# RWKV scan on one core: the inversion's matrix is made ahead of the other latent products, the two halves of a join run together, and the first heads' output projection stands ahead of the last chain

## The chip, the core and the metric

The kernel runs on one core of a Trainium2 chip. A core has five engines that each take their instructions in a fixed order: TensorE (PE in the profile; PEld is its loading of weights), VectorE (DVE), ScalarE (ACT), GpSimd (POOL) and SyncE (SP, which issues most of the transfers). The metric is the time of one execution in microseconds (us) on the device; lower is better.

## The reference

Two transformer blocks of two layers each, at 256 tokens by 1024 channels, all in float32; the second block also has 256 context tokens. The change concerns one mixer of the second block's last layer, the RWKV-7 scan over 16 heads of 64 channels, with a context part and then a latent part, in both directions:

```python
def rwkv7_scan(r, w, k, v, kk, a, S):
    def step(S, inp):
        rt, wt, kt, vt, kkt, at = inp
        sa = jnp.einsum("bhvk,bhk->bhv", S, -kkt)
        S = S * wt[:, :, None, :] + sa[..., None] * (kkt * at)[:, :, None, :] + vt[..., None] * kt[:, :, None, :]
        return S, jnp.einsum("bhvk,bhk->bhv", S, rt)
    S, ys = lax.scan(step, S, xs)

def rwkv_out(y, p, kvec, lnx, w_o):
    y = head_layernorm(from_heads(y), lnx[0], lnx[1], RW_HEADS, r.dtype)
    bonus = jnp.sum((r * k * kvec[2]).reshape(bn, L, RW_HEADS, RW_HEAD), axis=-1, keepdims=True) * v...
    return ((y + bonus.reshape(bn, L, D)) * g) @ w_o
```

The latent scan of each direction starts from that direction's final context state. Only the latent output goes on (`need_ctx` is false in the last layer).

## The kernel before

The scan is computed in chunks of 64 tokens. With N the strictly triangular 64x64 matrix of a chunk's keys against their own decayed keys, the chunk needs the inverse of (1 + N). The 16 heads go in four batches, g = 0 to 3, of four heads: two planes (`pl`) of 128 channels, each with two heads. A batch has 64 such matrices (4 heads, 2 directions, 4 chunks, context and latent). Its stages are:

- `prepare(lat)`, for the context (lat 0) and then the latent part (lat 1). `scaled_keys` makes the decays and the scaled keys: small matmuls at L1561, L1575 and L1578 with 64 or fewer rows, a tanh, a scan on VectorE, two exponentials, and elementwise products. `products` then makes, in runs of 64x64 matmuls at L1626, the keys against the rates (one kind gives N, copied by ScalarE at L1633 into the tile XN, the other kind gives A12, masked by VectorE at L1632), for the latent part also the keys against the receptances (masked by VectorE into AL, L1645), and the keys by token (transposes, copied by ScalarE into BT, L1648). `values` transposes the values (L1661) into SV (L1664). The latent part also makes the bonus (L1590 to L1593).
- `invert_blocks`: two copies on ScalarE (L1678), a transpose on VectorE (L1680, tile `ul`), and 62 VectorE operations (L1688, L1690) that invert all 32x32 diagonal blocks of the batch at once. It reads XN of both parts alone.
- `join_blocks`: the blocks are joined to inverses of 64x64 by two rounds of 32x32 matmuls (L1712, L1717), each with copies behind it (L1714, L1719), first for one half of the units, then for the other. Ahead of it ScalarE moves the off-diagonal blocks (L1701).
- `chain(lat)`: four steps, each of which waits for the one before: matmul pp (L1753), copy P, matmul pu (L1760), copies SV on ScalarE and VectorE (L1762), matmul pd (L1765), scaling on VectorE (L1769). The latent chain also adds up the output py (L1742).
- `output`: head layer norm, bonus and gate (L1786 to L1812).

At the end `finish` multiplies by `w_o`: weights are loaded and split into a high and a low part (L209 on ScalarE, L210 on VectorE), and each of 8 output tiles is a sum of matmuls of three products (L242, L243, L244). The first six chunks of channels (batches 0 to 2) are summed early, 8 times 18 matmuls; the last two after batch 3's output.

The order on each engine comes from the Tile framework: it emits instructions by priority, which is the order of the program unless a block is wrapped in `C.early(mark)`, and takes one that is ready by its own plan. So the order is fixed when the kernel is built. The program's order was: all of batch g+1's `prepare(0)`, then batch g's chain(0), `prepare(1)` of g+1, then the inversion of g+1 with chain(1) of g wrapped early, the join, the output of g. `finish` is emitted after both chains of batch 3. PSUM has two banks for the small matmuls (`psm`), two for products, joins and the projection (`ptr`), and one each for the chain's pp, pu, pd and py.

## Time and profile before

| | before |
|---|---|
| median of 3 runs | 2874.9 us (2871.64 to 2876.14) |
| profiled execution | 2889.15 us |
| its span, first to last instruction | 2887.3 us |
| granted TensorE clock, mean of the span | 0.914 |
| busy: TensorE, VectorE, ScalarE | 90%, 72%, 45% of the span |
| the RWKV scan, from batch 0's first key to batch 3's output | 2137.3 to 2652.8 us |

The median is of runs without the profiler; the rows below are all from the one profiled execution, so lengths of stages are to be held against 2889.15. A granted clock of 1.00 is TensorE's 2.4 GHz, 0.50 is 1.2 GHz; a mean between them is a mix of both.

### The profile page before, as it was taken

How to read it: one execution, taken by the hardware profiler on the slowest of the kernel's cores; microseconds unless marked ns; L12 is line 12 of the kernel's file. 1: busy time of each engine (PE TensorE's matmuls, PEld its weight loads, DVE VectorE, ACT ScalarE, POOL GpSimd, SP SyncE). 2: the span in 40 equal slices, each digit the busy share in tenths (PEclk: the TensorE clock that was granted, in tenths of full speed). 3: DMA queues.
4: the chain of work that ended last, by engine and by line, in shares of the span. 5: the costliest groups of instructions: out<-in, count | busy, mean ns of one | idle time of the engine just before them, and what ended most of it. 6: DMA issues, size and time to landing. Idle time of an engine off the chain costs nothing. (4 is left out here: it accounts for less than half of the span.)

```text
span 2887.3 us, 52999 instructions
## 1 busy us (share of the span) xinstructions
PE 2602.2 (90%) x21548; PEld 2303.9 (80%) x21548; DVE 2065.4 (72%) x4032; ACT 1286.7 (45%) x2237; POOL 632.1 (22%) x417
## 2 busy tenths in 40 slices
PE   8988989999989999899996999897995887788898
PEld 8987889999978899887865877676873766665898
DVE  7785877877866888555438997987858576733993
ACT  5443454444444454346444432335753343322564
POOL 1042320220333301320104212123012010101443
PEclk9998999999989999999986999998995876866899
DMA  7663236666643266521102445432320000011454
GB/s 243 210 217 99 88 112 215 212 214 202 219 156 103 90 211 212 168 88 45 52 30 83 134 153 188 162 117 97 122 75 14 9 18 9 28 38 44 146 187 135
DMA packets 315891, 356.86 MB, mean 124 GB/s; under 512 B 9088, under 2 KB 294016, under 8 KB 315520
## 3 DMA queue, kind: packets, MB, share of 16 engines
q1 hardware_dynamic: 315648, 353.47, 37.7%
q8 instruction: 170, 2.79, 0.4%
q14 instruction: 73, 0.60, 0.1%
HBM read 348.20 MB, written 5.24 MB: 122 GB/s over the span
## 5 line engine op out<-in xcount | busy, mean ns | idle before, releaser
L242 PE MATMUL pmm<-x,hi 128*128 128x256 f32 (+1 forms) x2944 | 927.3, 317 | 39.3 <-ACT hi L209 9.8
L243 PE MATMUL pmm<-x,hi 128*128 128x256 f32 (+1 forms) x2944 | 921.3, 313 | 9.2 <-DVE x L920 5.7
L244 PE MATMUL pmm<-x,lo 128*128 128x256 f32 (+1 forms) x2944 | 918.3, 312 | 1.9 <-DVE lo L210 1.9
L209 ACT ACTIVATE hi<-raw 128x1024 fp32r<-128x1024 f32 (+3 forms) x572 | 570.6, 1002 | 706.5 <-PE pmm L243 406.6
L210 POOL TENSOR_TENSOR lo<-raw,hi 128x1024 fp32r<-128x1024 f32 (+3 forms) x191 | 443.9, 2325 | 1448.5 <-ACT hi L209 1358.3
L242 PEld LDWEIGHTS pmm<-x,hi 128*128 128x128 f32 x2944 | 563.6, 192 | 84.7 <-issue 16.4
L210 DVE TENSOR_TENSOR lo<-raw,hi 128x1024 fp32r<-128x1024 f32 (+2 forms) x381 | 475.8, 1250 | 200.1 <-ACT hi L209 197.9
L243 PEld LDWEIGHTS pmm<-x,hi 128*128 128x128 f32 x2944 | 562.8, 191 | 49.7 <-DVE x L920 8.0
L244 PEld LDWEIGHTS pmm<-x,lo 128*128 128x128 f32 x2944 | 563.0, 191 | 38.9 <-issue 4.2
L242 PE MATMUL pmm<-ah,hi 128*128 128x256 f32 (+1 forms) x1056 | 319.6, 303 | 16.0 <-DVE X L332 11.7
L244 PE MATMUL pmm<-ah,lo 128*128 128x256 f32 (+1 forms) x1056 | 318.9, 302 | 2.5 <-DVE lo L210 2.5
L243 PE MATMUL pmm<-al,hi 128*128 128x256 f32 (+1 forms) x1056 | 318.3, 301 | 0.0
L242 PEld LDWEIGHTS pmm<-ah,hi 128*128 128x128 f32 x1056 | 201.6, 191 | 25.8 <-issue 18.1
L882 DVE SCALAR_TENSOR_TENSOR modp<-wmod,cond 128x512 bf16<-128x512 f32 (+1 forms) x210 | 199.3, 949 | 27.4 <-DMA wmod<-in_w_mod_dram 25.7
L244 PEld LDWEIGHTS pmm<-ah,lo 128*128 128x128 f32 x1056 | 201.5, 191 | 10.8 <-DVE lo L210 3.0
L243 PEld LDWEIGHTS pmm<-al,hi 128*128 128x128 f32 x1056 | 201.7, 191 | 7.8
L1280 DVE SCALAR_TENSOR_TENSOR cv<-pmm,vecs,cv 128x189 f32<-128x189 f32 (+3 forms) x396 | 154.5, 431 | 1.9
L882 DVE SCALAR_TENSOR_TENSOR modp<-wmod,X 128x1024 bf16<-128x1024 f32 x78 | 114.6, 1470 | 23.8 <-DMA wmod<-in_w_mod_dram 22.7
L283 PE MATMUL pmm<-hi,x 128*128 128x256 f32 x224 | 67.9, 303 | 0.0
L1294 ACT ACTIVATE cv<-cv 128x512 f32<-128x512 f32 (+1 forms) x44 | 22.9, 524 | 99.6 <-DVE cv L1280 99.5
L285 PE MATMUL pmm<-lo,x 128*128 128x256 f32 x224 | 66.6, 297 | 0.0
L284 PE MATMUL pmm<-hi,x 128*128 128x256 f32 x224 | 66.3, 296 | 0.0
(495 smaller groups left out, 4010.1 us busy)
## 6 DMA issues: line engine op xcount, KB each, us to landing
raw<-in_ffn_w_up_dram SPq DMA_DIRECT2D x88, 1024.0 KB, 5.4
raw<-in_ffn_w_gate_dram SPq DMA_DIRECT2D x44, 1024.0 KB, 5.4
raw<-in_ffn_w_down_dram SPq DMA_DIRECT2D x40, 896.0 KB, 4.6
raw<-in_ffn_w_down_dram SPq DMA_DIRECT2D x28, 1024.0 KB, 5.3
raw<-in_w_in_dram SPq DMA_DIRECT2D x28, 1024.0 KB, 5.2
wmod<-in_w_mod_dram SPq DMA_DIRECT2D x48, 512.0 KB, 6.2
wmod<-in_w_mod_dram SPq DMA_DIRECT2D x96, 256.0 KB, 2.7
raw<-in_ev_w_in_dram SPq DMA_DIRECT2D x14, 1024.0 KB, 5.2
```

Source lines behind the costliest of these rows:

```text
L209: self.last_split = self.nc.scalar.activation(hi, src, AF.Copy)
L210: (eng or self.nc.vector).tensor_tensor(lo, src, _f(hi), op=ALU.subtract)
L242: mm(out, wh, xh, start=start, stop=False)
L243: mm(out, wh, xl, start=False, stop=False)
L244: mm(out, wl, xh, start=False, stop=stop)
L283: mm(out, xh[:, a], wh[:, j, :n], start=k == 0, stop=False)
L284: mm(out, xl[:, a], wh[:, j, :n], start=False, stop=False)
L285: mm(out, xh[:, a], wl[:, j, :n], start=False, stop=k == nk - 1)
L882: nc.vector.scalar_tensor_tensor(t, w, 1.0, self.room[:, 4 * q + n * h:4 * q + n * (h + 1)], op0=ALU.mult, op1=ALU.mult, accum_out=part[:, ...
L1280: nc.vector.scalar_tensor_tensor(dst, src, cw(i, m), dst, op0=ALU.mult, op1=ALU.add)
L1294: nc.scalar.activation(t, t, AF.Gelu_apprx_tanh)
```

## The change

- A batch's preparation is cut in three. `context()` makes all of the context part. `latent()` makes the latent scaled keys and only that kind of the products that gives N. `rest()` (the other kind with its mask A12, AL, BT, values and bonus) is emitted behind the inversion.
- The four small matmuls of `scaled_keys` stand together, two on rows 0 to 63 and two on rows 64 to 127 of the same weight tiles: the key norms are now spread over the channels by 64 one-hot rows beneath `rw_a2`, which takes the place of the matmul at L1575, and each pair writes two banks.
- The join runs round one for both halves, then round two for both. VectorE makes the copies that ScalarE made at L1701, and half of those behind round two.
- `finish` becomes the class `RwkvOut`: the early sums over six channel chunks are emitted ahead of batch 3's chain(0), the loading and splitting of the last two chunks' weights ahead of its chain(1) (not shown in the diff).
- The bonus product is written over R.r; its pool of wide tiles has four buffers where it had three.

```diff
             batches = [RwkvBatch(C, R, sp, tp, 0)]
-            for lat in range(2):
-                batches[0].prepare(lat)
+            batches[0].context()
+            batches[0].latent()
             batches[0].invert_blocks()
+            batches[0].rest()
             batches[0].join_blocks()
             for g, batch in enumerate(batches):
                 if g < 3:
                     batches.append(RwkvBatch(C, R, sp, tp, g + 1))
-                    batches[g + 1].prepare(0)
+                    ahead = batches[g + 1]
+                    ahead.context()
+                else:
+                    out = RwkvOut(batch, X, mv)
+                    out.over_first_heads()
                 batch.chain(0)
                 if g < 3:
-                    batches[g + 1].prepare(1)
+                    ahead.latent()
                 mark = C.tc.cur_priority
                 if g < 3:
-                    batches[g + 1].invert_blocks()
+                    ahead.invert_blocks()
+                else:
+                    out.split_last()
                 with C.early(mark):
                     batch.chain(1)
                 if g < 3:
-                    batches[g + 1].join_blocks()
-                    batch.output()
-            C.tp, C.width, C.squares = tp, S, 2
-            return batches[3].finish(X, mv, rms[1])
+                    ahead.rest()
+                    ahead.join_blocks()
+                batch.output()
+            return out.finish(rms[1])
...
-    def prepare(self, lat):
+    def tiles(self):
         for tag, tiles, bufs in (("BT", self.BT, 4), ("A12", self.A12, 4), ("SV", self.SV, 3)):
             tiles.append(self.stacked(tag, bufs))
-        keys = [self.scaled_keys(lat, pl) for pl in range(2)]
+
+    def context(self):
+        self.tiles()
+        keys = [self.scaled_keys(0, pl) for pl in range(2)]
         for pl in range(2):
-            self.products(lat, pl, keys[pl])
+            self.keys_by_rates(0, pl, keys[pl], 2)
+            self.keys_by_token(0, pl, keys[pl])
+        for pl in range(2):
+            self.values(0, pl)
+
+    def latent(self):
+
+        self.tiles()
+        self.keys = [self.scaled_keys(1, pl) for pl in range(2)]
+        for pl in range(2):
+            self.keys_by_rates(1, pl, self.keys[pl], 0)
+
+    def rest(self):
+        for pl in range(2):
+            self.keys_by_rates(1, pl, self.keys[pl], 1)
+            self.keys_by_receptances(pl, self.keys[pl])
+            self.keys_by_token(1, pl, self.keys[pl])
+        for pl in range(2):
+            self.values(1, pl)
+            self.bonus(pl)
...
-        th, px = wide("th"), C.psm()
+        th, one, two = wide("th"), C.psm(), C.psm()
+        pa, pk = one[:, S:], two[:, S:]
         nc.gpsimd.memset(th[:, :, :, 0], 0.0)
-        for z in range(2):
-            zr = slice(64 * z, 64 * z + 64)
-            p = px[:, z * S:(z + 1) * S]
-            nc.tensor.matmul(p, self.w2[zr, ch], R.tw[zr, a], start=True, stop=True)
-            nc.scalar.activation(th[:, z, :, 1:], steps(flip(p, z)), AF.Tanh, scale=0.5,
+        for c, w, v in ((0, self.w2, R.tw), (S, self.a2, R.ta)):
+            for zr, p in ((slice(0, 64), one), (slice(64, 128), two)):
+                nc.tensor.matmul(p[:, c:c + S], w[zr, ch], v[zr, a], start=True, stop=True)
+        for z, p in enumerate((one, two)):
+            nc.scalar.activation(th[:, z, :, 1:], steps(flip(p[:, :S], z)), AF.Tanh, scale=0.5,
...
-        pk = C.psm()
-        nc.tensor.matmul(pk[:, :S], C.cst("headrow")[64 + 32 * (m // 4):72 + 32 * (m // 4), (m % 4) * P:(m % 4 + 1) * P],
-                         R.rows[m // 4][:, a], start=True, stop=True)
-        pa = pk[:, S:]
-        nc.tensor.matmul(pa, self.a2[:64, ch], R.ta[:64, a], start=True, stop=True)
         kk = tile("kk")
-        nc.vector.scalar_tensor_tensor(kk, k0, col("rw_kvec0"), pk[:, :S], op0=ALU.mult, op1=ALU.mult)
+        nc.vector.scalar_tensor_tensor(kk, k0, col("rw_kvec0"), pk, op0=ALU.mult, op1=ALU.mult)
...
-        if lat:
-            rk = tile("rk")
-            nc.vector.scalar_tensor_tensor(rk, R.r[:, m], R.hk[:, m:m + 1], kf, op0=ALU.mult, op1=ALU.mult)
-            pb = C.psm()
-            nc.tensor.matmul(pb[:, :S], C.cst("headones"), rk, start=True, stop=True)
-            nc.vector.tensor_tensor(R.bv[:, m], pb[:, :S], R.vl[:, m], op=ALU.mult)
...
+            nc.vector.scalar_tensor_tensor(R.r[:, m], R.r[:, m], R.hk[:, m:m + 1], kf, op0=ALU.mult, op1=ALU.mult)
...
+    def keys_by_rates(self, lat, pl, bks, kind):
+
+        C, nc, A12 = self.C, self.C.nc, self.A12[lat]
+        kinds = (0, 1) if kind == 2 else (kind,)
+        banks = {i: self.bank() for i in kinds}
+        self.times(bks, lambda eo, i: banks[i], lambda rr, z, s, eo: A12[rr, z, pl, s, eo], kinds)
+        if 1 in banks:
+            strict = C.cst("strict").unsqueeze(1).unsqueeze(1)
+            for eo, rr in ((0, slice(64, 128)), (1, slice(0, 64))):
+                nc.vector.tensor_tensor(A12[rr, :, pl, :, eo], banks[1][rr], strict[rr].to_broadcast([64, 2, 4, 64]), op=ALU.mult)
+        if 0 in banks:
+            nc.scalar.activation(self.XN[:, lat, :, pl], banks[0], AF.Copy, scale=0.5)
...
         for low in (slice(32, 64), slice(96, 128)):
-            nc.scalar.activation(N[low, :, 32:], N[low, :, :32], AF.Copy)
+            nc.vector.tensor_copy(N[low, :, 32:], N[low, :, :32])
             nc.gpsimd.memset(N[low, :, :32], 0.0)
-        for half in range(2):
-            us = range(16 * half, 16 * half + 16)
-            sl = slice(16 * half, 16 * half + 16)
-            wq, wx = C.ptr(), C.ptr()
-            pq, px = (t.rearrange("p (u t) -> p u t", t=32) for t in (wq, wx))
-            qt = tp.tile([P, 16, 32], F32, tag="qt", name=C.nm("qt"), bufs=1)
-            rows = [(slice(64 * eo, 64 * eo + 32), slice(64 * eo + 32, 64 * eo + 64)) for eo in range(2)]
-            for u in us:
+        rows = [(slice(64 * eo, 64 * eo + 32), slice(64 * eo + 32, 64 * eo + 64)) for eo in range(2)]
+        halves = [(slice(16 * i, 16 * i + 16), C.ptr().rearrange("p (u t) -> p u t", t=32)) for i in range(2)]
+        for us, p in halves:
+            for u in range(16):
                 for lo, hi in rows:
-                    nc.tensor.matmul(pq[hi, u - 16 * half], N[lo, u, 32:], zt[lo, u], start=True, stop=True)
+                    nc.tensor.matmul(p[hi, u], N[lo, us.start + u, 32:], zt[lo, us.start + u], start=True, stop=True)
             for lo, hi in rows:
-                nc.scalar.activation(qt[hi], pq[hi], AF.Copy, scale=-1.0)
-            for u in us:
+                nc.scalar.activation(qt[hi, us], p[hi], AF.Copy, scale=-1.0)
+        for us, p in halves:
+            for u in range(16):
                 for lo, hi in rows:
-                    nc.tensor.matmul(px[lo, u - 16 * half], qt[hi, u - 16 * half], N[hi, u, 32:], start=True, stop=True)
+                    nc.tensor.matmul(p[lo, u], qt[hi, us.start + u], N[hi, us.start + u, 32:], start=True, stop=True)
             for lo, hi in rows:
-                nc.scalar.activation(N[lo, sl, 32:], px[lo], AF.Copy)
+                if us.start:
+                    nc.vector.tensor_copy(N[lo, us, 32:], p[lo])
+                else:
+                    nc.scalar.activation(N[lo, us, 32:], p[lo], AF.Copy)
...
+    def over_first_heads(self):
+        C, R, nc, w, early = self.C, self.R, self.C.nc, self.w, self.EARLY
+        self.raws, xl, los, xh = [self.room("A12", 4) for _ in range(2)], self.room("BT", 4), self.room("BT", 4), self.room("SV", 3)
+        his = [self.batch.sp.tile([P, 2, 4, 2, 64], F32, tag="AL", name=C.nm("AL"), bufs=4).rearrange("p z s a t -> p (z s a t)") for _ in range(2)]
+        cut = lambda t: t[:, :early * P].rearrange("p (k c) -> p k c", k=early)
+        self.xs = [(xh[:, m * S:(m + 1) * S].bitcast(F32R), xl[:, m * S:(m + 1) * S].bitcast(F32R)) for m in range(NKC)]
+
+        self.y = [R.bv[:, m] if m < early else self.batch.tp.tile([P, S], F32, tag=f"s{S}", name=C.nm("y"), bufs=4) for m in range(NKC)]
         for m in range(early):
-            C.split(*xs[m], R.y[:, m])
+            C.split(*self.xs[m], R.y[:, m])
         for pair in range(NKC // 2):
-            raw = cut(raws[pair % 2][:, :early * 2 * P], early)
+            raw = self.raws[pair % 2][:, :early * 2 * P].rearrange("p (k c) -> p k c", k=early)
             nc.sync.dma_start(raw, w[:early * P, pair * 2 * P:(pair + 1) * 2 * P].rearrange("(k p) c -> p k c", p=P))
             for i in range(2):
-                hi, lo = (cut(t[i][:, :early * P], early).bitcast(F32R) for t in (his, los))
+                hi, lo = (cut(t).bitcast(F32R) for t in (his[i], los[:, 1024 * i:]))
                 C.split(hi, lo, raw[:, :, i * P:(i + 1) * P])
                 ps = C.ptr()[:, :S]
-                C.dense_t(ps, (hi, lo), xs[:early])
-                nc.scalar.activation(y[2 * pair + i], ps, AF.Copy)
-        raw = cut(raws[0], 2)
-        nc.sync.dma_start(raw, w[early * P:].rearrange("(k p) c -> p k c", p=P))
-        hi, lo = (cut(t, 2).bitcast(F32R) for t in (hi2, lo2))
-        C.split(hi, lo, raw, nc.gpsimd)
-        old = raws[1].rearrange("p (m n) -> p m n", m=NKC)
-        nc.sync.dma_start(old, R.xd)
-        self.output()
+                C.dense_t(ps, (hi, lo), self.xs[:early])
+                nc.scalar.activation(self.y[2 * pair + i], ps, AF.Copy)
```

**TensorE at the scan's end, before.** The rows are from the last chain: L242 to L244 are the projection's matmuls (`ptr`), L1742 (py) and L1760 (pp, pu) those of the chain.

```order
L1742 MATMUL py_26291<-AR_21366,SV_25275 64x64 x3
L1760 MATMUL pp_26349<-P_26360,XN_24836 64x64
L1760 MATMUL pu_26350<-P_26360,XN_24836 64x64
L242 MATMUL ptr_26596<-SV_26511,AL_26508 128x256
L1760 MATMUL pp_26349<-P_26360,XN_24836 64x64
L243 MATMUL ptr_26596<-BT_26505,AL_26508 128x256
L1760 MATMUL pu_26350<-P_26360,XN_24836 64x64
L244 MATMUL ptr_26596<-SV_26511,BT_26509 128x256
L1760 MATMUL pp_26349<-P_26360,XN_24836 64x64
```

**TensorE at the same place now**: the end of the early projection and the first chain steps of batch 3 (L1783 is the former L1760, L1788 the former L1765, L1776 the former L1753, L1771 the former L1748).

```order
L244 MATMUL ptr_26282<-SV_26105,BT_26104 128x256
L242 MATMUL ptr_26282<-SV_26105,AL_26107 128x256
L243 MATMUL ptr_26282<-BT_26103,AL_26107 128x256
L244 MATMUL ptr_26282<-SV_26105,BT_26104 128x256
L1783 MATMUL pu_26303<-P_26313,XN_24816 64x64
L1788 MATMUL pd_26304<-SV_24824,BT_24822 64x64 x8
L1776 MATMUL pp_26343<-SV_24824,A_4244_24823 64x64 x8
L1771 MATMUL pd_26345<-SV_24824,ident 64x64 x8
```

The 144 projection matmuls now stand together ahead of the second half of the first step; from there to the end of the chain there are only chain matmuls on the engine.

**TensorE while batch 3's blocks are inverted, before**: only batch 2's latent chain is there (L1753, L1748, L1742, L1760).

```order
L1753 MATMUL pp_24547<-SV_22689,A_3973_22688 64x64
L1742 MATMUL py_24432<-AR_21365,SV_22689 64x64
L1753 MATMUL pp_24547<-SV_22689,A_3973_22688 64x64 x7
L1748 MATMUL pd_24549<-SV_22689,ident 64x64 x8
L1742 MATMUL py_24432<-AR_21365,SV_22689 64x64 x3
L1742 MATMUL py_24432<-AR_21366,SV_22689 64x64 x4
L1760 MATMUL pp_24547<-P_24558,XN_22250 64x64
L1760 MATMUL pu_24548<-P_24558,XN_22250 64x64
```

**TensorE there now**: batch 2's chain (L1776 is pp, L1765 py) with the moved products of batch 3 (L1636, the former L1626).

```order
L1776 MATMUL pp_24358<-SV_22681,A_3967_22680 64x64
L1765 MATMUL py_24186<-AR_21363,SV_22681 64x64
L1636 MATMUL ptr_24489<-A_4132_23967,bk_24036 64x64 x5
L1776 MATMUL pp_24358<-SV_22681,A_3967_22680 64x64
L1636 MATMUL ptr_24489<-A_4132_23967,bk_24036 64x64
L1776 MATMUL pp_24358<-SV_22681,A_3967_22680 64x64
```

The products went behind the inversion's start and stand between the chain's matmuls, one by one in places. Counted in the built order from the start of a join to the next, changes between matmuls of different tile shape (128x128, 128x64, 64x128, 64x64, 32x32) were 51 up to the first join, then 43, 66 and 61, and 183 behind the last; they are now 20, 80, 122, 111 and 25.

**TensorE at batch 3's join, before**: round one is L1712, round two L1717, with the chain's first matmuls between them.

```order
L1712 MATMUL ptr_25941<-zt_25722,XN_24836 32x32 x32
L1717 MATMUL ptr_25942<-XN_24836,qt_25943 32x32 x32
L1712 MATMUL ptr_26012<-zt_25722,XN_24836 32x32 x32
L1760 MATMUL pp_26127<-P_26138,XN_24836 64x64 x4
L1760 MATMUL pu_26128<-P_26138,XN_24836 64x64 x4
L1717 MATMUL ptr_26013<-XN_24836,qt_26014 32x32 x32
L1765 MATMUL pd_26129<-SV_24844,BT_24842 64x64 x8
```

**TensorE there now**: L1731 is round one, L1737 round two; L1827 and L1829 belong to batch 2's output.

```order
L1731 MATMUL ptr_25919<-zt_25470,XN_24816 32x32 x32
L1731 MATMUL ptr_25920<-zt_25470,XN_24816 32x32 x32
L1827 MATMUL psm_26089<-rows_26087,consts_all 128x256
L1829 MATMUL psm_26090<-rsg,kv_26057 128x256
L1737 MATMUL ptr_25919<-XN_24816,xs_25374 32x32 x32
L1737 MATMUL ptr_25920<-XN_24816,xs_25374 32x32 x32
L1829 MATMUL psm_26090<-rsg,kv_26057 128x256
```

Both halves of a round now stand together, and the chain's matmuls come behind.

## Rows read from the trace of the kernel before

**Rows 1.** Part 1 of the page: each engine's busy time, share of the span and instructions.

```profile
PE 2602.2 (90%) x21548; PEld 2303.9 (80%) x21548; DVE 2065.4 (72%) x4032; ACT 1286.7 (45%) x2237; POOL 632.1 (22%) x417
```

**Rows 2.** Stretches between batches: start:end, length, busy time by engine, granted clock, DMA.

```profile
2137.30:2197.40 60.10, 52.68 (x753) 39.21 (x754) 39.84 (x66) 31.14 (x63) 15.32 (x30) 0.69 0.07 20
2197.40:2237.60 40.20, 13.56 (x120) 7.43 (x120) 38.96 (x93) 10.25 (x22) 15.59 (x11) 0.57 0.04 12
2237.60:2290.20 52.60, 45.95 (x1268) 41.32 (x1270) 19.83 (x37) 24.40 (x44) 2.99 (x4) 0.84 0.04 11
2290.20:2325.20 35.00, 23.48 (x394) 17.38 (x396) 32.59 (x90) 5.72 (x13) 0.92 (x5) 0.81 0.02 5
2325.20:2393.90 68.70, 62.30 (x1323) 50.98 (x1324) 41.59 (x73) 35.37 (x70) 13.95 (x19) 0.77 0.06 17
2393.90:2430.60 36.70, 24.17 (x374) 17.49 (x373) 33.88 (x93) 6.17 (x14) 1.59 (x6) 0.78 0.02 5
...
2571.60:2638.90 67.30, 67.18 (x352) 45.34 (x350) 6.81 (x12) 9.54 (x17) 4.52 (x1) 0.63 0.09 32
```

**Rows 3.** Chain of waits ahead of batch 3's inversion: start us, length us, engine, tile, line.

```profile
2494.12 2.23 PE ptr L1626 x54
...
2499.17 1.99 DVE ul L1680
```

**Rows 4.** The same chain of waits through batch 3's join.

```profile
2536.34 1.94 PE ptr L1712 x64
...
2538.91 1.05 ACT XN L1701
...
2546.68 1.84 PE ptr L1717 x64
```

**Rows 5.** TensorE's timeline where dense and chain matmuls alternate, at two granted clocks.

```profile
2573.06 0.39 PE L243 MATMUL ptr<-BT,AL 128*128 128x256 f32 x1
...
2573.63 0.39 PE L244 MATMUL ptr<-SV,BT 128*128 128x256 f32 x1
...
2597.87 0.58 PE L242 MATMUL ptr<-SV,AL 128*128 128x256 f32 x1
...
2598.79 0.58 PE L243 MATMUL ptr<-BT,AL 128*128 128x256 f32 x1
```

**Rows 6.** TensorE's timeline where dense matmuls stand next to each other.

```profile
2565.82 0.28 PE L243 MATMUL ptr<-BT,AL 128*128 128x256 f32 x1
2565.94 0.27 PE L244 MATMUL ptr<-SV,BT 128*128 128x256 f32 x1
```

**Rows 7.** A stretch of the last two chains, with the columns of rows 2.

```profile
2580.00:2620.00 40.00, 40.00 (x144) 25.61 (x144) 3.19 (x5) 5.04 (x8) 4.52 (x1) 0.50 0.08 27
```

**Rows 8.** VectorE's timeline: one copy in each chain step, context, then latent.

```profile
2270.92 0.43 DVE L1762 COPY SV<-pu 64x256 f32<-64x256 f32 x1 [1.35 <-PE pu L1760]
...
2275.01 0.43 DVE L1762 COPY SV<-pu 64x256 f32<-64x256 f32 x1 [2.02 <-PE pu L1760]
...
2296.95 0.43 DVE L1762 COPY SV<-pu 64x256 f32<-64x256 f32 x1
...
2301.82 0.43 DVE L1762 COPY SV<-pu 64x256 f32<-64x256 f32 x1
```

**Rows 9.** Chain of waits at the scan's end: the last operation of batch 3's output.

```profile
2652.82 0.70 DVE X L1812
```

**Rows 10.** Groups by line and shape on VectorE, 2137 to 2540 us: count, busy, mean ns, idle.

```profile
L1632 DVE TENSOR_TENSOR A<-ptr,consts_rwkv 64x512 f32<-64x512 f32 x32 | 22.0, 687 | 15.2 <-PE ptr L1626 14.8
...
L1645 DVE TENSOR_TENSOR AL<-ptr,consts_rwkv 128x512 f32<-128x512 f32 x16 | 10.5, 677 | 3.1 <-PE ptr L1626 3.1
```

**Rows 11.** TensorE's timeline: one run of the 64x64 product matmuls.

```profile
2501.78 1.68 PE L1626 MATMUL ptr<-ident,bk 64*64 64x64 f32 x61 [0.73 <-DVE AL L1645]
```

**Rows 12.** TensorE's timeline: two matmuls on different halves of the rows.

```profile
2143.89 0.48 PE L1561 MATMUL psm<-rtw,w 64*128 64x256 f32 x1
2143.89 0.48 PE L1578 MATMUL psm<-rta,a 64*128 64x256 f32 x1
```

More of the change, by code (lines that the diff above doesn't have):

```diff
@@ L1371, in __init__ @@
         self.sg = t("rsg", [S])
-        self.rows = [self.ta[r:r + 8] for r in (64, 96)]
         self.I = I
@@ L1541, in scaled_keys @@
         nc = C.nc
-        self.values(lat, pl)
         A12 = self.A12[lat]
@@ new lines, in times, with bank @@
+        for z in range(2):
+            for s in range(4):
+                for i in kinds:
+                    for eo, rr, partner in heads:
+                        self.C.nc.tensor.matmul(banks(eo, i)[partner if i else rr, z, s], bks[z][rr, s, i], other(rr, z, s, eo), start=True, stop=True)
+    def bank(self):
+        return self.C.ptr().rearrange("p (z s t) -> p z s t", z=2, s=4)
+    def keys_by_rates(self, lat, pl, bks, kind):
[9 more added lines that the diff above has]
+            nc.scalar.activation(self.XN[:, lat, :, pl], banks[0], AF.Copy, scale=0.5)
```

105 lines of the change are left out of this document (49 added, 56 removed).

## The prediction

> **What bounds the kernel now.** The page's first part says that TensorE is busy for 90% of the span [rows 1], but the change touches only the scan, and there the limit alternates. So I read the stretches between the landmarks of each batch (start of the join, start of `ul`, start of the next join) [rows 2]. The fifth row is batch 2's preparation with batch 1's context chain beside it: TensorE 62.3 of 68.7 us, VectorE 41.6. The sixth is the inversion of the same batch with batch 1's latent chain: VectorE 33.9 of 36.7 us, TensorE 24.2. Batch 3's pair of stretches repeats it (68.6 and 37.1 us from the starts of L1680 and L1712 in [rows 3, 4] and the end of the sixth row). So the preparation is bound by TensorE, the inversion by VectorE, and each leaves the other engine room. Then the chain of waits: what ends last before `ul` is a run of L1626 products [rows 3], and most of those that stand in this stretch don't feed N. Through the join the chain goes from TensorE to ScalarE and back, 2536.34 to 2548.52, 12.2 us [rows 4]. Last the end of the scan: TensorE is busy 67.2 of 67.3 us, at a mean clock of 0.63 (the last row of [rows 2]). Its timeline there is one projection matmul, two matmul records of the chain, one projection matmul [rows 5].
>
> **The costs.** All sums are against the profiled execution, 2889.15 us; the median of 2874.9 is 14.2 below it, and I take off the same at the end.
>
> *The moved products.* A run of 61 records of L1626 takes 1.68 us at full clock [rows 11]; a product leaves two records, so a run of 32 products is about 1.7 us. `rest()` has 160 products and 32 transposes of values per batch, six such runs: 10.2 us of TensorE at full clock, 20 at half. VectorE's part is four masks L1632 of 0.69 and four L1645 of 0.68 [rows 10], 5.5 us, and two small products of the bonus that I estimate at under 1 us together, from their half size.
>
> *Batch 0.* Nothing runs beside its preparation, so taking `rest()` out shortens it by the products at the clock of this stretch, 0.69: 10.2 / 0.69 = 15, and by some of the masks for which the bank turns wait, 5: 60.1 becomes 40. The inversion behind it has VectorE busy 39.0 of 40.2 (the second row of [rows 2]), so whatever VectorE gets there is added: 5.5 of masks and about 3.5 of the next context's scaled keys, which the built order now puts ahead of the join. Net -20 + 9 to 10 = **-10**. Bounds: -16 if only the masks come back, 0 if the shortening is only the 10 us of the products at full clock.
>
> *Cycles 1 to 3.* Each preparation loses 10.2 us of products at a clock of 0.77 to 0.84, 12 to 13 us, on the engine that bounds it; VectorE's 41.6 is the floor at which this stops, far below. The join gets shorter by about 3 (by [rows 4] two runs of L1712 in a row 3.9, a copy 0.6, two of L1717 3.7, a copy 0.6, so 9 for 12.2); the copies that went from ScalarE (1.05 each) to VectorE aren't in the trace in that form; by L1632's 512 columns in 0.69 [rows 10] I estimate 1024 at 1.4 at most and half of it at least, which is under 1 us for the pair either way. But the scaled-key matmuls of the next context, which stood ahead of the join, now stand behind it, and the join's copies wait in VectorE's queue: +3 to 4. That they now go in pairs on different rows, which can start together (both at 2143.89 in [rows 12]), returns under 1 us. So the preparation gives -12. The inversion gets 5.5 to 6.4 of VectorE work less what it leaves over, and here a second price counts. Where projection and chain matmuls alternate, one pair takes 2573.63 - 2573.06 = 0.57 us at full clock and 0.92 at half [rows 5]. A projection matmul among its like takes 0.12 [rows 6], and the chain's two records about 0.11 (an estimate: 0.028 for a record in [rows 11], where two heads go side by side, so 0.055 alone); so each of the two changes costs (0.57 - 0.12 - 0.11) / 2 = 0.17, and with both doubled at half clock 0.23. The built order has 37, 56 and 50 changes more in the cycles of the inversions: 6 to 13 us of TensorE each. With 24.2 + 11.5 + 10 = 46 TensorE passes VectorE's 33.9 + 6 = 40, so I add 8 to each inversion, not 5. Net -12 + 8 = -4 each, **-12**. Bounds per cycle: -10 (VectorE alone decides) and +7 (all that TensorE gets is late).
>
> The Trainium skill, page "TensorEngine Tiling (Array Packing)", section Key Properties, states that changing the tiling mode, and not just the tile, drains the engine. The trace agrees: 0.57 us for what would be 0.23 without changes [rows 5, 6]. The page gives no price; by its rule alone 143 changes more in the inversions and 158 fewer at the end would nearly cancel, by the rows they don't, as the first lie half under VectorE's work and the last on the path.
>
> *The end.* Now 2536.3 to 2638.9, 102.6 us, from join to last step. Instead: the join 9; two splits of batch 2's output before the first matmul 1.5; 144 projection matmuls at 0.12, 17 at full clock and about 33 at twice that, taken as 22 as these stand without a gap at first at full clock; eight chain steps alone. A context step takes 2275.01 - 2270.92 = 4.1 us and a latent one 4.87 [rows 8], so 36; I take 42, since the clock in the inversions, where such a chain stood nearly alone, was 0.78 to 0.81 and not 1. The sum is 74.5, **-28**. Bounds: -39 (9 + 1.5 + 17 + 36) and -6 (join and splits 11, projection 33, eight steps at 6.6, by half the clock for the TensorE part of a step). The loads of the weights move ahead with the block on SyncE's queue and land beside the last inversion and the join, where the transfer engines are 2 to 9% busy (the next to last number of each row in [rows 2]); the splits lie beside the projection. But all of the chain is now queued behind the block on TensorE: if the block waits for a weight or for batch 2's output, each us of it is a us of the end. The output behind the last step, 2638.9 to 2653.5 [rows 2, 9], stays.
>
> *At nothing:* the new class, the fourth wide buffer, the bonus written in place (its wait for GpSimd's reading of R.r lies hundreds of instructions ahead of the next use; if that cover goes, 1 to 2 us a batch), 64 rows more of a weight load per batch.
>
> Sum: -10 - 12 - 28 = -50, so 2839 in the profile and **2825** for the median.
>
> **The rivals.**
>
> - *Forecast*, 55%: 2825, its own range 2805 to 2845.
> - *The inversions give all back*, 17%. TensorE becomes the bound there and `rest()` takes as long as it saved. For it speak the 46 against 40 above; against it that TensorE's idle time there is 12.5 us now. The cycles then give 0, batch 0 -5, end -28: -33, **2842**.
> - *The last chain alone runs at half clock*, 10%. For it: the clock was 0.50 for 40 us in this place already [rows 7], and chain steps leave TensorE idle. Against it: in these 40 us TensorE was busy for all 40, so idleness isn't what took the clock down, and in the inversions with TensorE busy two thirds it was near 0.8. End -6, the rest -22: -28, **2847**. The Trainium skill, page "TensorE: Matmul & The Clock Gate", section "What's actually happening", says that "the default state is throttled, and activity releases the throttle", which speaks for this rival; the trace doesn't agree with it there [rows 7].
> - *More than that*, 12%. VectorE decides in all cycles (-10 each), and the end is at its bound of -38, batch 0 -12: -80, **2795**.
> - *Slower*, 6%. In the inversions the alternation takes the clock to 0.5, as at the end before. Then TensorE's 24.2 at 0.78 becomes 38, the moved products 20, 50 changes at 0.23 another 12: 70 against 36.7, +33 in each of three, +99, less 36 in the preparations, less 5 and 28: +30, **2905**. It decides from a stretch of 60 us on.
>
> **How the numbers follow.** The time is that of the forecast. The range, 2790 to 2862, reaches over the second and third rival and into the larger gain; left out are the slower case and the outer parts of the others, about 2 in 10. A change within 0.2%, 5.7 us, is about what a measurement of this kernel can't tell from none. Faster is all of the first four but their upper tails, 0.89; same 0.04, from the tails of the second and third; slower 0.07.
>
> **What would show it.** In the profile after: `ul` of batch 0 begins about 40 us after its first key (now 60.1); preparations of about 56 us; inversions of 43 to 46 with TensorE busy over 40 and VectorE about 40; a join of 9 us; 144 projection matmuls in one block of 17 to 33 us; eight steps of 4 to 6 us with no other matmul between; scan's end about 50 us earlier. It would be wrong if inversions last over 55 us, if the block waits for weights or for batch 2's output, or if the steps last over 6 us.

## The result and the profile after

The changed kernel takes 2835.06 us (median of 3 runs, 2829.34 to 2838.16) against 2874.9: ratio 0.9861, 95% interval 0.9833 to 0.9889, so 40 us less where 50 were forecast. Two further measurements beside other runs of the kernel before gave 0.9795 (0.9733 to 0.9856) and 0.9812 (0.9786 to 0.9839). The profiled execution has a span of 2833.2 us, 54.1 under that of before; 10.1 of these lie ahead of the scan's first key (2127.2 for 2137.3 us), where the change touches almost nothing, so the stages are compared from there on. The page's first part, after [rows 1]:

```profile
PE 2576.5 (91%) x21548; PEld 2305.7 (81%) x21548; DVE 2073.0 (73%) x4047; ACT 1272.3 (45%) x2220; POOL 633.2 (22%) x417
```

The stretches of batches 1 to 3 in the changed kernel, with the columns of [rows 2]: inversion 1, preparation 2, inversion 2, preparation 3, inversion 3.

```profile
2250.80:2300.20 49.40, 41.95 (x752) 35.35 (x753) 36.48 (x98) 9.76 (x21) 0.79 (x4) 0.77 0.01 2
2300.20:2355.30 55.10, 51.18 (x1026) 41.46 (x1026) 39.26 (x72) 28.65 (x61) 14.14 (x20) 0.74 0.08 24
2355.30:2413.00 57.70, 51.34 (x668) 40.92 (x668) 34.47 (x96) 9.34 (x20) 0.92 (x5) 0.69 0.01 2
2413.00:2462.70 49.70, 47.47 (x975) 39.19 (x976) 39.06 (x68) 28.42 (x58) 16.61 (x19) 0.71 0.12 35
2462.70:2522.80 60.10, 51.22 (x716) 41.15 (x717) 38.31 (x104) 12.46 (x28) 0.00 (x0) 0.67 0.09 28
```

Preparations went from 68.7 and 68.6 to 55.1 and 49.7, as meant. But an inversion that took 36.7 us with VectorE busy for 33.9 takes 57.7, with VectorE still at 34.5: the growth in busy time is TensorE's, 24.2 to 51.3. What TensorE did there shows in its timeline, in inversion 3:

```profile
2475.11 0.33 PE L1765 MATMUL py<-AR,SV 128*64 128x64 f32 x2
2475.37 0.33 PE L1636 MATMUL ptr<-ident,bk 64*64 64x64 f32 x2
2475.62 0.33 PE L1765 MATMUL py<-AR,SV 128*64 128x64 f32 x2
```

One chain matmul, one moved product (each leaves two records), and 0.26 us from each to the next. In a block, 61 records of the product take 1.68 us [rows 11], 0.055 for two. A little later the products take turns with chain matmuls of their own shape, 64x64, and there the starts lie 0.01 to 0.1 us apart; at half clock the alternation of unlike shapes takes 0.40 a step:

```profile
2478.96 0.27 PE L1636 MATMUL ptr<-ident,bk 64*64 64x64 f32 x1
2478.97 0.27 PE L1783 MATMUL pp<-P,XN 64*64 64x64 f32 x1
2478.98 0.27 PE L1636 MATMUL ptr<-ident,bk 64*64 64x64 f32 x1
...
2490.05 0.47 PE L1636 MATMUL ptr<-A,bk 64*64 64x64 f32 x2
2490.45 0.47 PE L1765 MATMUL py<-AR,SV 128*64 128x64 f32 x2
```

Why does more work on TensorE lengthen a stretch in which VectorE has no more to do than before? VectorE's operations that invert the blocks read none of the products, but its fixed order has the masks of the products and the chain's copies between them. In inversion 2 of the changed kernel, a mask between two steps of the inversion:

```profile
2377.20 0.42 DVE L1711 TENSOR_TENSOR xt<-ul,xs 128x252 f32<-128x252 f32 x1
2384.99 0.69 DVE L1650 TENSOR_TENSOR A<-ptr,consts_rwkv 64x512 f32<-64x512 f32 x1 [7.37 <-PE ptr L1636]
2385.72 0.42 DVE L1713 TENSOR_TENSOR xs<-xs,xt 128x252 f32<-128x252 f32 x1
```

All of VectorE's waits for TensorE in this stretch are 21.7 us; in the kernel before they are 1.1. The longest of the changed kernel (waiter, releaser: us in total, times, longest), then all of the kernel before:

```profile
DVE A L1650 <- PE ptr L1636: 7.4, 1, 7.4
DVE SV L1785 <- PE pu L1783: 3.8, 1, 3.8
DVE AL L1659 <- PE ptr L1636: 3.7, 3, 2.5
```
```profile
DVE ul L1680 <- ACT XN L1678: 1.3, 1, 1.3
DVE v L1795 <- PE psm L1793: 1.1, 1, 1.1
```

Then comes the clock; the first three rows below are from inversion 3, the other three the join, the projection block and the chain at the end:

```profile
2468.00:2474.00 6.00, 6.00 (x149) 5.29 (x150) 5.09 (x15) 0.76 (x2) 0.00 (x0) 1.00 0.02 3
2480.00:2504.00 24.00, 23.96 (x291) 19.66 (x288) 11.30 (x26) 4.67 (x9) 0.00 (x0) 0.50 0.11 34
2504.00:2522.00 18.00, 9.79 (x123) 7.66 (x117) 13.45 (x47) 5.87 (x13) 0.00 (x0) 0.59 0.14 44
2522.80:2533.00 10.20, 10.20 (x263) 8.68 (x263) 5.55 (x8) 3.53 (x6) 2.44 (x2) 0.50 0.01 3
2537.00:2552.50 15.50, 15.50 (x135) 15.08 (x134) 5.75 (x6) 7.47 (x14) 0.00 (x0) 0.99 0.37 123
2554.00:2584.80 30.80, 24.28 (x559) 20.45 (x558) 9.15 (x22) 7.09 (x16) 4.52 (x1) 1.00 0.04 16
```

The clock fell to 0.50 (1.2 GHz) in the alternation, with TensorE busy for 23.96 of 24 us, and went back to full (0.99) in the block of projection matmuls. It stayed at 1.00 through the chain alone, with TensorE busy for 24.3 of 30.8. The chain's steps by VectorE's copy, a context and a latent pair [rows 8]:

```profile
2557.86 0.43 DVE L1785 COPY SV<-pu 64x256 f32<-64x256 f32 x1 [1.96 <-PE pu L1783]
2561.95 0.43 DVE L1785 COPY SV<-pu 64x256 f32<-64x256 f32 x1 [2.02 <-PE pu L1783]
...
2570.47 0.43 DVE L1785 COPY SV<-pu 64x256 f32<-64x256 f32 x1 [2.35 <-PE pu L1783]
2574.93 0.43 DVE L1785 COPY SV<-pu 64x256 f32<-64x256 f32 x1 [2.35 <-PE pu L1783]
```

4.1 and 4.5 us a step. The stages of all kernels, from the starts of `ul` and `zt` in VectorE's timeline: batch 0 is from the first scaled-key matmul to its `zt`, the cycles from there to batch 3's `zt` (join, preparation and inversion of batches 1 to 3), the end from there to the start of the last operation of batch 3's output. us of one profiled execution each, with the ratio to the kernel before in runs beside it:

| kernel | batch 0 | cycles 1-3 | end | sum | ratio (95%) |
|---|---|---|---|---|---|
| before | 98.4 | 298.8 | 118.4 | 515.5 | 1 |
| changed | 87.9 | 305.8 | 76.4 | 470.0 | 0.986 (0.983-0.989) |
| changed, second | 85.8 | 301.9 | 76.4 | 464.1 | 0.980 (0.973-0.986) |
| changed, third | 85.8 | 301.9 | 76.4 | 464.0 | 0.981 (0.979-0.984) |
| late projection | 88.4 | 305.4 | 98.8 | 492.7 | 0.987 (0.983-0.991) |
| rest in blocks | 84.8 | 257.8 | 76.1 | 418.8 | 0.962 (0.959-0.966) |
| rest in blocks, again | 89.1 | 258.0 | 76.2 | 423.3 | 0.969 (0.967-0.972) |
| rest behind chain | 84.8 | 262.3 | 77.2 | 424.3 | 0.963 (0.960-0.966) |
| join by halves | 85.8 | 312.5 | 77.8 | 476.0 | 0.978 (0.974-0.982) |
| blocks, keys one by one | 85.9 | 275.2 | 76.5 | 437.6 | 0.974 (0.969-0.979) |
| blocks, batch 0 too | 87.1 | 259.1 | 77.2 | 423.4 | 0.968 (0.963-0.974) |
| projection alone | 99.1 | 300.9 | 76.0 | 476.1 | 0.988 (0.982-0.994) |
| blocks, N not first | 89.2 | 270.1 | 75.9 | 435.2 | 0.971 (0.969-0.973) |
| neither | 92.3 | 270.3 | 79.1 | 441.5 | 0.975 (0.973-0.978) |

The runs of the kernel before, one slow run left out, spread from 2866 to 2908 us beside one of these sets, more than the 0.2% of the prediction, so small steps are read from the stages. These differ by up to 4 us between executions of one and the same kernel (batch 0 of the kernel in blocks, 84.8 and 89.1), so that steps under this aren't told apart either.

### The profile page after: what moved, and what is told of

Same layout as the page of the kernel before. It is cut to its first block, busy times and chain, and to the rows that moved or that the text cites. A ratio compares the mean times of both kernels' runs of the same rounds, so it can differ in the third digit from the quotient of the medians.

```text
span 2833.2 us, 53019 instructions
## 1 busy us (share of the span) xinstructions
PE 2576.5 (91%) x21548; PEld 2305.7 (81%) x21548; DVE 2073.0 (73%) x4047; ACT 1272.3 (45%) x2220; POOL 633.2 (22%) x417
## 5 line engine op out<-in xcount | busy, mean ns | idle before, releaser
L242 PE MATMUL pmm<-x,hi 128*128 128x256 f32 (+1 forms) x2944 | 930.6, 318 | 35.7 <-ACT hi L209 9.8
L244 PE MATMUL pmm<-x,lo 128*128 128x256 f32 (+1 forms) x2944 | 922.2, 314 | 3.9 <-DVE lo L210 3.9
L242 PEld LDWEIGHTS pmm<-x,hi 128*128 128x128 f32 x2944 | 566.5, 193 | 81.6 <-ACT hi L209 14.0
L244 PEld LDWEIGHTS pmm<-x,lo 128*128 128x128 f32 x2944 | 565.6, 192 | 41.2 <-DVE lo L210 4.8
L242 PE MATMUL pmm<-ah,hi 128*128 128x256 f32 (+1 forms) x1056 | 318.0, 301 | 15.7 <-DVE X L332 11.9
L244 PE MATMUL pmm<-ah,lo 128*128 128x256 f32 (+1 forms) x1056 | 317.5, 301 | 3.1 <-DVE lo L210 3.1
L242 PEld LDWEIGHTS pmm<-ah,hi 128*128 128x128 f32 x1056 | 199.8, 189 | 25.9 <-issue 18.1
L244 PEld LDWEIGHTS pmm<-ah,lo 128*128 128x128 f32 x1056 | 200.2, 190 | 12.0 <-DVE lo L210 4.0
L1294 ACT ACTIVATE cv<-cv 128x512 f32<-128x512 f32 (+1 forms) x44 | 22.9, 523 | 90.0 <-DVE cv L1280 89.9
```

The costliest lines, as they stand in the source:

```text
L242: mm(out, wh, xh, start=start, stop=False)
L244: mm(out, wl, xh, start=False, stop=stop)
```

## The experiments

Two theories of why the cycles gave nothing. The first: the moved products stand one by one between chain matmuls of another tile shape, and each change costs, the more so as the clock falls. The second: it is the amount of work behind the inversion's start, wherever it stands there. Others test single terms of the sum.

**The projection late again.**

```diff
-                else:
-                    out = RwkvOut(batch, X, mv)
-                    out.over_first_heads()
                 batch.chain(0)
...
-                else:
-                    out.split_last()
                 with C.early(mark):
                     batch.chain(1)
...
+                else:
+                    out = RwkvOut(batch, X, mv)
+                    out.over_first_heads()
+                    out.split_last()
                 batch.output()
```

> The changed kernel, but the 144 early projection matmuls and the last weights' split are emitted behind batch 3's two chains again, so that they stand between the chain's matmuls. From the two profiles the end, join to last step, went from 102.7 to 62.0 us and the output behind it from 14.4 to 13.1. First theory: all of this is the order of the projection, so the time returns to 2835 + 39 = 2874 us, within 5. Second theory: the profiled run before was 14 us above the median, and the end is worth only the 28 us that were forecast: 2863 us.

2857.15 us, where the kernel before took 2893.92 (0.9866): neither number. Its end is 98.8 us, 22 more than with the block, but 20 less than in the kernel before, with alternating matmuls in both. The two orders are not quite the same: counted in the traces, the end has 163 changes of tile shape here and 181 in the kernel before, which at the prediction's 0.17 to 0.23 us each makes 3 to 4 us (an estimate). Most of the difference is the clock. The same 20 us in the kernel before, and then in this one:

```profile
2576.30:2596.30 20.00, 20.00 (x80) 13.03 (x76) 2.96 (x5) 1.62 (x4) 0.00 (x0) 0.55 0.15 53
```
```profile
2576.30:2596.30 20.00, 20.00 (x115) 13.28 (x115) 2.76 (x4) 4.41 (x6) 4.52 (x1) 0.97 0.15 53
```

**The projection alone**, on the kernel before:

```diff
+                else:
+                    out = RwkvOut(batch, X, mv)
+                    out.over_first_heads()
                 batch.chain(0)
...
+                else:
+                    out.split_last()
                 with C.early(mark):
                     batch.chain(1)
...
```

The class `RwkvOut` comes with it (not shown).

> The kernel before with one part of the change: the 144 early projection matmuls ahead of batch 3's chain(0), and the last weights' split ahead of its chain(1). The join stays by halves. First theory (the alternation at the end costs 0.17 us for each of 158 changes, and more when the clock falls to 0.50 with it): the end becomes 65 to 68 us. In the profile of the kernel before it was 102.7, in that of the kernel with the late projection 83.8 at a clock that stayed near 1.00 for 20 us longer; so 17 to 38 us less, ratio 0.987 to 0.994. Second theory (a chain alone loses the clock, and the block is added to it): end of 95 us or more, ratio over 0.997.

The end is 76.0 us for 118.4 (from join to last step 62.3 for 102.7), and 2846.2 us for 2879.5, a ratio of 0.988: the first theory, with an end 3 us shorter than it gave. All other stages stayed (99.1 and 300.9). So the end's 42 us in the profile are the projection's order, and it is worth 22 to 42, mostly by what the clock did in the run it is held against.

**The rest emitted ahead of the inversion** in batches 1 to 3:

```diff
                     ahead.latent()
+                    ahead.rest()
...
-                    ahead.rest()
                     ahead.join_blocks()
```

> The changed kernel, but for batches 1 to 3 the rest of the latent products is made ahead of the inversion again (batch 0 keeps it behind). Changes of tile shape fall from 79, 123 and 110 in the three cycles to 44, 55 and 55. In the two profiles cycles 2 and 3, join to join, went from 105.4 and 105.7 us to 112.8 and 109.8, cycle 1 from 87.6 to 83.2. First theory (the moved products cost more behind the inversion's start than they saved ahead of it): cycles of 84, 102 and 102 us, that is those of before less the shorter join, so 17 us less than the changed kernel, 2818 us. Second theory (cycles 2 and 3 got longer for another reason, such as the scaled keys that now stand behind the join): no better than 2835 us, or worse by the 19 us that the preparations had gained.

2786.19 us, better than either theory gave. The trace tells why: the inversion starts as soon as N is there, whatever is emitted next, so the rest still runs behind its start. The products (L1636) in inversion 2, where the columns are records, duration min/median/max in ns, and first and last start; in the changed kernel:

```profile
L1636 PE MATMUL ptr<-ident,bk x128: 218/311/367, 2364.6 to 2397.0; 64*64 64x64 f32 x128
L1636 PE MATMUL ptr<-AR,bk x106: 218/311/367, 2356.8 to 2393.6; 64*64 64x64 f32 x106
L1636 PE MATMUL ptr<-A,bk x32: 311/312/367, 2376.6 to 2384.6; 64*64 64x64 f32 x32
```

and in this kernel:

```profile
L1636 PE MATMUL ptr<-ident,bk x128: 217/219/268, 2338.8 to 2348.6; 64*64 64x64 f32 x128
L1636 PE MATMUL ptr<-AR,bk x91: 217/219/268, 2338.2 to 2346.6; 64*64 64x64 f32 x91
L1636 PE MATMUL ptr<-A,bk x32: 218/219/267, 2341.8 to 2342.9; 64*64 64x64 f32 x32
```

266 records in 40 us there, 251 in 10.4 here, ahead of the latent chain. The stretch, in the columns of [rows 2]:

```profile
2338.40:2374.70 36.30, 27.39 (x685) 23.77 (x680) 33.25 (x86) 9.13 (x20) 0.79 (x4) 0.98 0.01 2
```

685 TensorE records in 27.4 us at a clock of 0.98; the changed kernel had 668 in 51.3 at 0.69. So emission decided the mixture, not the side of the inversion's start.

**The rest in the chain's banks**, so that it comes behind the chain:

```diff
+    def room(self):
+        if self.turn is None:
+            return self.C.ptr()
+        self.turn += 1
+        tag = ("pp", "pu", "pd", "py")[self.turn % 4]
+        return self.C.pch.tile([P, 512], F32, tag=tag, name=self.C.nm(tag))
+
+    turn = None
+
...
     def rest(self):
+        if self.g:
+            self.turn = 3
...
-        return self.C.ptr().rearrange("p (z s t) -> p z s t", z=2, s=4)
+        return self.room().rearrange("p (z s t) -> p z s t", z=2, s=4)
...
-        pv = C.ptr().rearrange("p (z s c) -> p z s c", z=2, s=4)
+        pv = self.room().rearrange("p (z s c) -> p z s c", z=2, s=4)
```

> The changed kernel, but for batches 1 to 3 the rest of the latent products takes the chain's four PSUM banks in turn, so that its products can't begin before the chain's last step has given them up. They then stand in blocks behind the chain and not between its matmuls; work and engine shares are the same. Changes of tile shape are 39, 59 and 53 in the three cycles, where they were 79, 123 and 110. First theory (the alternation costs: 0.26 us for each change at full clock and 0.40 at half, and the clock of 0.50 that went with it): the inversions of 49, 58 and 60 us become 40 to 45, bound by VectorE's 34 to 38, so 30 to 38 us less, 2797 to 2805 us. Second theory (the amount of moved work costs, wherever it stands in the inversion): inversions still of 50 to 60 us, 2830 to 2840 us; if the wait for the chain's banks is added, over 2840.

2789.5 us, with inversions (`ul` to `zt`) of 36.4, 37.2 and 38.1. Inversion 2:

```profile
2349.00:2388.20 39.20, 30.06 (x689) 24.82 (x688) 34.21 (x95) 9.00 (x20) 0.91 (x5) 0.89 0.01 3
```

The same amount, behind the chain instead of ahead of it, and again VectorE is busy for most of the stretch, 34.2 of 39.2 us. Its waits for TensorE are 3.1 us here and 0.9 with the rest ahead, for 21.7 in the changed kernel. This shows the first theory against the second: blocks on either side do, the mixture costs 40 to 48 us over three cycles. How much of this is the price of the changes, how much the lower clock beside them, no run separates.

**The rest in blocks, again**, beside the changed kernel and the next one.

> The kernel of the second run (rest emitted ahead of the inversion in batches 1 to 3) unaltered, to hold it against the changed kernel on one chip. Its trace shows that its rest still runs behind the inversion's start, but in blocks ahead of the chain: 251 records from 2338.2 to 2348.6 us, where the changed kernel has 266 from 2356.8 to 2397.0. First theory (only the alternation differs): 40 to 50 us less than the changed kernel beside it, as the profiles' 418.8 and 464.1 to 470.0 us from the first key to batch 3's output say. Second theory (the level of the chip made the difference): under 20 us less.

> The changed kernel unaltered beside the two others. Both theories: 40 to 50 us above the kernel with the rest in blocks if that one's gain is real; stretches as in its earlier traces, that is inversions 1 to 3 of 47, 52 to 56 and 58 us.

2788.1 against 2827.47 us: 39 less, just under what the first theory gave. The changed kernel's inversions were 47.4, 55.7 and 54.3 us, the last of them under the 58 expected. The changed kernel's other measurement stood beside three of the runs below:

> The changed kernel unaltered, beside the same runs of the kernel before as the three that follow, so that they can be held against it. If nothing differs between the chips but their level, its ratio to the kernel before is 0.986 again, within 0.004; if the level of the kernel before is more changeable than its own, 0.975 to 0.986.

0.9795, with an interval, 0.9733 to 0.9856, that takes in both. Inversion 2, which took 57.7 us at a clock of 0.69 above, is shorter in this execution of the same kernel, with the same 668 records, at a clock of 0.76:

```profile
2344.00:2397.80 53.80, 47.47 (x668) 38.19 (x668) 34.39 (x96) 9.29 (x20) 0.92 (x5) 0.76 0.01 2
```

**N not first**, in blocks: `latent()` makes all products of a plane.

```diff
-            self.keys_by_rates(1, pl, self.keys[pl], 0)
+            self.keys_by_rates(1, pl, self.keys[pl], 2)
+            self.keys_by_receptances(pl, self.keys[pl])
+            self.keys_by_token(1, pl, self.keys[pl])
...
```

> The kernel of the second run, but the latent products are made in the order of the kernel before: for each plane N and A12 together, then AL, then BT, so that batch's N is complete only when most of them are done. All other parts of the change stay (pairs, join, projection). First theory (N first lets the inversion start 10 us of products earlier): batch 0 becomes 8 to 12 us longer and each cycle 6 to 12, so 26 to 48 us more than with N first in blocks. Second theory (VectorE's scaled keys set the start of the inversion, and the pairs and the join gave the cycles' gain): within 10 us of it.

Between the theories: batch 0 89.2 (84.8 and 89.1 with N first), cycles 270.1 for 258, and 2794.95 us for 2788.1, with intervals that overlap. So N first is worth about 12 us over three cycles when it stands in blocks; in batch 0 it isn't told apart from nothing.

**Batch 0 in the same order.**

```diff
-            batches[0].invert_blocks()
             batches[0].rest()
+            batches[0].invert_blocks()
```

> As the kernel with the rest ahead of the inversion, but in batch 0 too, so that no batch makes it behind. First theory (behind the inversion's start it pays only where no chain stands beside it, as in batch 0, whose two stretches went from 100.3 to 89.7 us): 10 us slower than with batch 0's rest behind, ratio 0.965 to 0.967. Second theory (batch 0's gain is that of the pairs and of the other edits, not of the place of the rest): within 3 us of it, ratio 0.961 to 0.964.

Batch 0 takes 87.1 us, between the two values with its rest emitted behind (84.8 and 89.1), and the ratio isn't told apart. But this decides nothing about the place of the rest, as the edit didn't move it: N still comes first, and 248 records of the products run from 2181.9 to 2194.3 us, beside and behind the start of `ul` (2182.1), as they do where the rest is emitted behind. So neither theory was tested.

**Scaled keys one by one**, in blocks with N first:

```diff
-        for c, w, v in ((0, self.w2, R.tw), (S, self.a2, R.ta)):
-            for zr, p in ((slice(0, 64), one), (slice(64, 128), two)):
-                nc.tensor.matmul(p[:, c:c + S], w[zr, ch], v[zr, a], start=True, stop=True)
...
+        for z, zr in enumerate((lo, hi)):
+            p = px[:, z * S:(z + 1) * S]
+            nc.tensor.matmul(p, self.w2[zr, ch], R.tw[zr, a], start=True, stop=True)
+            nc.scalar.activation(th[:, z, :, 1:], steps(flip(p, z)), AF.Tanh, scale=0.5,
                                  bias=R.hv[:, z * NKC + m:z * NKC + m + 1])
+        pk, pa = C.psm()[:, :S], C.psm()[:, :S]
+        for p, zr in ((pk, hi), (pa, lo)):
+            nc.tensor.matmul(p, self.a2[zr, ch], R.ta[zr, a], start=True, stop=True)
```

> The kernel with the rest of the products ahead of the inversion (batches 1 to 3) once more, but the four scaled-key matmuls no longer go in pairs: the two for the decays share a bank with a tanh between them, and the key norms and the rates have a bank each. The work is the same. In the profiles these matmuls' records were busy for 62.0 us in the kernel before, one after another, and 38 us with pairs. First theory (the pairs are worth what their records lost, 6 us a batch, as they stand on the path of the preparation; the prediction had put them under 1 us): 20 to 30 us slower than with pairs, ratio to the kernel before 0.970 to 0.973. Second theory (the pairs are hidden as was forecast): within 5 us, ratio 0.962 to 0.964.

2803.86 us (0.974); in the stages 437.6 for 418.8 to 423.3, the first theory's sign and less than its size. 14 of the 17 us in the cycles are in the last one, whose preparation took 68.8 us at a granted clock of 0.68, where the kernel with pairs took 57.3 at 0.76.

**Neither pairs nor N first**, the same edit on the kernel with N not first:

> The kernel of the run before with all products in the old order (N not first), and the scaled-key matmuls not in pairs either; join, projection and the place of values and bonus stay as changed. First theory (pairs and N first are two ways to the same gain of batch 0, and the pairs make most of the cycles'): batch 0, whose two stretches took 98.4 us in the kernel before, 89.2 with pairs alone and 85.9 with N first alone, goes back to 95 to 99; the three cycles, 270.1 with pairs alone and 275.2 with N first alone, to 284 to 292 (298.8 before, less the join's 9). In all 20 to 30 us more than with the pairs, ratio 0.979 to 0.983. Second theory (values and bonus behind the products, or the join, made the gain): batch 0 stays below 92 and the cycles below 278, ratio under 0.976.

2808.22 us (0.975). The first theory falls, and the second holds but for 0.3 us of batch 0: cycles 270.3, where they are 270.1 with pairs, batch 0 92.3. Beside the 298.8 and 98.4 of before, 28 and 6 us are gained without pairs, N first or the projection.

**The join by halves again**: one half of the tile between the rounds for both.

```diff
-                nc.scalar.activation(qt[hi, us], p[hi], AF.Copy, scale=-1.0)
+                nc.scalar.activation(qt[hi, :16], p[hi], AF.Copy, scale=-1.0)
```

> The changed kernel, but both halves of a join share one half of the tile between the rounds, so that the second half's copy waits until the first half's second round is done, as in the kernel before. First theory (the join stands on the path alone): 1 to 2.5 us more for each of four joins, 2839 to 2845 us. Second theory (other work fills the join): within 2 us of 2835.

Inconclusive in time (2824.62 us, 0.978; the changed kernel 0.980 to 0.986), neither theory's number. In the stages the stretches from `zt` to `ul` are 41.5, 60.6 and 51.8 us for 35.7, 57.2 and 51.7, so 9 us of cycles, and the end is 1.4 longer.

## Why the prediction was right, step by step

The time lies 10 us over the forecast, but that it came so near is luck: the cycles came out 19 us worse than forecast and the end 14 us better.

- *Batch 0, -10*: -10.5 (98.4 to 87.9). The split held nearly as well: `ul` 35.7 us after the first key (40 forecast), and from there to the join 54.1 (49 forecast). Its reason didn't hold alone: without N first and without pairs it is already 92.3, 6 of the 10.5.
- *Cycles, -12*: +7.0 in the profile (305.8 for 298.8; +3.1 in the two others). The step that failed is "I add 8 to each inversion", an overlap that wasn't there. From `ul` to `zt` they grew by 15.7, 23.6 and 22.9 us; inversions 2 and 3 lasted 57.7 and 60.1 to the join, over the 55 that the prediction had named as a sign of being wrong. The busy times were sized nearly right: TensorE 42.0, 51.3 and 51.2 us (46 forecast), VectorE 36.5, 34.5 and 38.3 (40 forecast). But I let half of TensorE's growth lie under VectorE's work, and the runs showed VectorE standing still in inversion 2 for 21.7 us until TensorE had made a product or a chain step (1.1 before), as its order puts masks and copies between the steps of the inversion. In blocks, with the same work, it waits 0.9 us and the stretch takes 36.3. The price of a change was a smaller miss: 0.20 us at full clock and 0.29 at half (0.26 and 0.40 less about 0.055 and 0.11 of the matmul's own) for 0.17 and 0.23. So was their number: counted in the traces, 45, 72 and 65 more from `ul` to `zt`, where I took the whole cycles' 37, 56 and 50, which the preparations' losses had made smaller. The clock of 0.50 in the longer alternations was the mechanism of the slower rival; its turning point, a stretch of 60 us, was just reached in inversion 3. The preparations gave 19, 15 and 22 (54.5, 72.1 and 73.2 to 35.7, 57.2 and 51.7 from `zt` to `ul`) where 12 were forecast.
- *"At nothing"*: wrong in sum. In the kernel with neither pairs nor N first, batch 0 and the cycles together are 35 us under before. Of it the join explains some 9 (forecast 3 each, measured 5.8, 3.4 and nothing from cycle to cycle). The values and the bonus behind the products, the fourth wide buffer, the key norms over 64 rows and the new place of the scaled keys are left; which of them it is wasn't tried and stays open. The traces show what no longer stands ahead of `ul`: in batch 0, 64 records of the values' transposes for 128 and 32 of the scaled-key matmuls for 42; in cycle 2, again 64 of the values for 128, with TensorE busy 60.4 us of 62.8 for 65.0 of 72.0.
- *Pairs, under 1 us*: 17 us over three cycles in one comparison (14 of them in a preparation at a lower clock), none in the other; in batch 0 none and 3, less than one kernel's batch 0 differs by. Not a fixed price.
- *The end, -28*: -42 with the output (-41 from join to last step), past its own bound of -39. The mechanism was right, the term mis-sized: I took 42 us for the chain, 22 for the block and 9 for the join. The chain took 31 us for seven and a half steps, as the clock was 1.00 and not 0.8, the block 20.6 (2532.8 to 2553.4 us), its first 4 us at half clock, and the join 10.
- *Last chain at half clock* is refuted by the row of 2554.0 us: 1.00 with a chain alone. By the rule of the page "TensorE: Matmul & The Clock Gate" of the Trainium skill, section "What's actually happening", that activity releases the throttle, this needn't have surprised in the block (0.50 to 0.99); the 24 us at 0.50 with TensorE busy throughout don't follow from busy time as the profile counts it.
- *The drain on a change of tiling mode*, which the Trainium skill states in "TensorEngine Tiling (Array Packing)", section Key Properties, agrees with the trace: 0.26 us from start to start between 128x64 and 64x64, 0.01 to 0.1 where matmuls of two tiles are both 64x64. By that rule alone the changes added and removed would nearly cancel; they didn't, as the end kept its 42 us, but the cycles gave back all of theirs, as the second rival had it.

The better version is the kernel with the rest emitted ahead of the inversion: 0.962 and 0.969 of before, 39 us under the changed kernel beside the same runs.

## What to carry to other kernels

When work is moved behind another chain's start, look at how the built order mixes the two on TensorE: single matmuls of different tile shape that take turns took several times their own time here, and in most of these stretches the clock was low as well. Emitting the moved block ahead, or giving it banks that make it wait for the chain's end, gave back 40 to 48 us of the three cycles at no cost in work. Idle time on one engine is also no room for more work if the engine that bounds the stage has operations in its queue that wait for this work: look for them before taking an overlap into the sum.

## What the runs showed of the hardware

- The granted clock went to 0.50 in 24 us in which TensorE was busy throughout with alternating shapes, and was 1.00 in a chain with 79% busy. Alternation doesn't always go with a low clock: with the late projection, TensorE alternates from 2576.3 to 2596.3 us, busy throughout, at 0.97.
- With one order of matmuls, inversion 2 of the changed kernel ran at a clock of 0.69 in one execution and at 0.76 in another, and took 57.7 us and 53.8.
- From one alternating matmul to the next it is 0.26 us at full clock and 0.40 at half, whichever of the two shapes (64x64 and 128x64) comes next. Matmuls of two tiles that have the same shape, 64x64, start 0.01 to 0.1 us apart when they take turns.
